# W_G's weight sums moved to the middle block's W_O, a fifth buffer for high halves, another order of k, and a product ahead of the last heads' attention

## The chip, the cores and the metric

The kernel runs on one core of a Trainium2 chip. The metric is the device time of one launch in microseconds, as the median of several runs. The engines are named PE (matrix products), DVE (vector), ACT (scalar), POOL (GpSimd) and SP (which here only issues transfers). Each engine works through its own instructions in program order; it waits on semaphores that the others, and the transfers, raise.

## The reference

One layer over 2112 tokens (2048 of a prompt and 64 of a sample, which start from states of their own), model width 1024, all in float32:

```
h = rms_norm(x, g_pre);  proj = h @ w_in            # ten column groups of 1024: vA bA cA zA q f iv zB gA gB
yA = (silu(zA) * bA * causal_conv3(cA * vA)) @ w_a_out                    # path a
S, o = hgrn2_scan(S0, silu(q) * scale, 1 - fg, iv, log(fg))               # path b: 8 heads, chunks of 64
yB = (norm(o) * g_onorm * silu(zB)) @ w_b_out
out = (sigmoid(gA) * yA + sigmoid(gB) * yB) @ w_o                         # W_O
x = x + rms_norm(out, g_post)
gate = sigmoid(rms_norm(x, g_ple) @ w_ple_gate)                           # W_G
x = x + (p @ w_ple_proj) * gate
```

Outputs are the new x of both sequences, the last two rows of the convolution's input and the last states of the scan.

## The kernel before

**Products.** A float32 product is made of three float32r products: every operand is split into a high half (an ACT cast) and a low half (a DVE subtraction, line 207), and PE adds high by high, high by low and low by high (lines 382 to 384 in sgroup, 549 to 551 in mm3). Most weight matrices are multiplied by a scheme of Strassen's kind: sgroup takes two column blocks of weights and needs seven products instead of eight, for which both sides need sums, four for the activations (T1 to T4, from operands) and four for the weights (S1 to S4, from prepare_sums). The rest (W_O in the first two blocks, a few heads) goes through mm3 directly.

**Blocks.** The tokens are cut into three blocks of 768, 704 and 640 columns, named first, middle and last here. Each block runs path_b (eight heads: head_prep makes the head's projections, head_attn its attention in steps), path_a (eight groups), merge (W_A, W_B and the gates), W_O (final_out), and final_norm. Between blocks the next one's operands are made: `operands` has four steps, i = 0 to 3, and each loads two tiles of x (x_fm, line 665, on POOL's queue), scales them (line 715), makes the sums (697 to 700) and splits them (207). `gates` yields the next block's first groups, sgroups that fill PE while final_norm's chain of small steps runs. In the last block W_O runs group by group inside the merge, and the gate product W_G of the middle and of the last block, which uses the sums of W_G, comes at the end.

**Weight sums.** prepare_sums(firsts, ahead) works group by group, four groups for each matrix. A group loads four weight tiles of 128 x 512 (line 339), makes S1, S3, S2 and S4 on DVE (lines 356, 358, 360, 362), stores each (345), splits it (ACT cast and DVE subtraction at 207) and stores its low half (348). All its transfers, 12 of 256 KB in each group, go through POOL's queue; without `ahead` the next group's loads come behind the former group's stores:

```
            if not ahead and n + 1 < len(groups):
                nxt = load(*groups[n + 1])
            yield
```

The generator is advanced by hooks. Before, path_a of the last block advances the one for W_G (`side`, from its group j = 3 on), as path_a of the middle block does for W_O.

**W_O of the middle block.** final_out calls gemms, which makes the outputs j = 0 and 1 together (gemm_late), 2 to 5 one by one, and 6 and 7 by k. Each output has two halves of 352 columns, and each takes eight k of three matmuls, 384 matmuls in all. The operand of k is the merged row block k; k = 3 and its neighbours are ready last, since the merge makes rows g and g + 4 together. `late` (3 here, 7 in the first block) tells gemm_late which k to leave to the end; that part is issued with the priority of a later place. The copies at line 1185 take the finished PSUM banks to xo[j], ACT squares them (660) and DVE adds the squares (661). At j = 1, 3, 5 and 7 one step of the next block's operands is issued.

**Order and buffers.** The program is written with generators and a list of hooks (`hooks`, `spread_out`): each product of a group calls one hook, which advances whatever stands first in the list; a None in it is a product with nothing attached. The framework then assigns buffers and orders each engine's instructions by priority. Weights come on SP's queue (line 217 the raw ones, 238 the stored low halves) into `raw` (5 buffers), are cast to `hi` on ACT (line 237; 4 buffers by the pool's default) and have their low half in `lo` (4) or `s` (3). `ring` holds 47 activation tiles ("r" in the profile) of 772 columns. PSUM has five banks for products (`pg`) and three for attention (`pa`). In head_attn the lines 951 and 953 are transposes on PE, which read what DVE made at 429.

Of the kernel before, what the change touches and what calls it, by code (L numbers as in the profile page):

```python
# [11 lines left out]
F32R = mybir.dt.float32r  # L12
# [6 lines left out]
P = 128  # L19
D = 1024  # L20
KB = D // P
# [11 lines left out]
W_A, W_B, W_O, W_G = 80, 88, 96, 104  # L33
# [3 lines left out]
CUT = SIZES[0] + SIZES[1] - DEC  # L37
BMAX = max(SIZES)
HMAX = BMAX // 2
RING = 47  # L40
HALVES = 9

LEAD = 7
# [40 lines left out]
def hybrid_step(  # L84
# [22 lines left out]
    wp = ctx.enter_context(tc.tile_pool(name="wp", bufs=4))  # L107
    ring = ctx.enter_context(tc.tile_pool(name="ring", bufs=RING))
# [7 lines left out]
    def nm(s):  # L116
        uid[0] += 1
        return f"{s}_{uid[0]}"
# [20 lines left out]
            yield  # L139

    def rt(n=None, dt=F32):
        return ring.tile([P, BMAX + 4], dt, tag="r", name=nm("r"))[:, : n or wide[0]]

    def hf(n=None):
        return ring.tile([P, HMAX], F32, tag="hf", name=nm("hf"), bufs=HALVES)[:, : n or wide[0] // 2]
# [85 lines left out]

    def split_w(raw, key=None, queue=SP):

        hi = wp.tile([P, 4, P], F32R, tag="hi", name=nm("hi"))
        if key in lows:
            lo = low_tile()
            A.copy(hi, raw)  # L237
            SP.dma_start(lo.bitcast(F32), lows[key])
            return hi, lo
        lo = wp.tile([P, 4, P], F32R, tag="lo", name=nm("lo"))  # L240
        split(raw, hi, lo)
        if key is not None:
            lows[key] = dram.tile([P, 4, P], F32, tag=f"lo{key}", name=nm("low"), bufs=1)
            queue.dma_start(lows[key], lo.bitcast(F32))
        return hi, lo
# [321 lines left out]
    def gemm_late(idxs, act, segs, late):  # L567

        ws = [load_w(i) for i in idxs]
        pss = [[ps_gemm() for _ in segs] for _ in idxs]  # L570
        ks = [k for k in range(KB) if k != late] + [late]
        for part in (ks[:-1], ks[-1:]):
            with placed() if len(part) == 1 else nullcontext():
                for row, w in zip(pss, ws):
                    for ps, s in zip(row, segs):
                        for k in part:
                            mm3(ps, w, act, k, cols_of(s), ks)
        return pss
# [460 lines left out]
    def path_b(bl, hc, first, kept, fills, hs):  # L1039


        def keep_z(hd, z):
            kept["o", hd] = spill("o", hd)
            G.dma_start(kept["o", hd], z)

        for hd in range(NH):
            d = head_prep(bl, hc, hd, first, hs)
            if not (first and hd == 0):
                next(fills, None)
            assert not hooks  # L1050
            attn = [head_attn(i, gs, d, hd) for i, gs in enumerate(bl["parts"])]
            hooks.extend([None] * 3 if first and hd == 0 else [])
            for step in range(4):
                hooks.extend(partial(next, g) for g in attn)
                if step == 2:
                    hooks.extend([None] * (2 if first and hd == 0 else 1))
            hooks.append(partial(keep_z, hd, d["z"]))
# [8 lines left out]
    def ple(bl, ph, kept, held=None, shared=False):  # L1066


        for j in range(KB):
            if held is not None:  # L1070
                hi, lo = held[j]
            else:
                raw = wp.tile([P, 4, P], F32, tag="raw", name=nm("raw"), bufs=5)[:, :2, :]
                SP.dma_start(raw, w_ple[j])
                with tc.high_priority():
                    hi = wp.tile([P, 4, P], F32R, tag="hi", name=nm("hi"))[:, :2, :]
                    lo = low_tile()[:, :2, :]
                    A.copy(hi, raw)
                    SP.dma_start(lo.bitcast(F32), lows["p", j])
            t = rt()  # L1080
            for s in bl["segs"]:
                pp, c = ps_attn()[:, : s["n"]], cols_of(s)
                for k, (xhi, xlo) in enumerate(ph):
                    T.matmul(pp, hi[:, k, :], xhi[:, c], start=k == 0, stop=False)
                    T.matmul(pp, hi[:, k, :], xlo[:, c], start=False, stop=False)
                    last[0] = T.matmul(pp, lo[:, k, :], xhi[:, c], start=False, stop=k == 1).ins
                with tc.high_priority():
                    if shared and j < 4 and s is bl["segs"][1]:
                        V.tensor_copy(t[:, c], pp)
                    else:  # L1090
                        copied = copies[0] = A.copy(t[:, c], pp).ins
            if bl["last"]:
                kept["p", j] = t
            else:
                kept["p", j] = spill("p", j)
                G.dma_start(kept["p", j], t)
                if not shared:
                    lows["p", j] = dram.tile([P, 2, P], F32, tag=f"lop{j}", name=nm("low"), bufs=1)
                    SP.dma_start(lows["p", j], lo.bitcast(F32))
            with behind_all((copied,) if hooks else ()):  # L1100
                hook()
            yield
# [298 lines left out]
    for bi, bl in enumerate(blocks):  # L1401
# [6 lines left out]
        nxt = None if bl["last"] else blocks[bi + 1]  # L1408
        cols, a_first = [], []
        rows = of_block(nxt, row_rstd(nxt, cols)) if nxt else iter(())  # L1410
        sums_ahead = prepare_sums((W_A, W_B), True) if first else prepare_sums((W_O,) if nxt else (W_G,), False)

        def side(rows, sums_):
            for j in range(KB):
# [42 lines left out]
        if nxt:  # L1457
            hc = new_operands()
            with width_of(nxt):
                ops = of_block(nxt, operands(hc, spread_all(cols), partial(load_x, nxt)))  # L1460
            for j, _ in enumerate(final_out(segs, mg, xo, acc, KB - 1 if first else KH - 1)):
                if j in (1, 3, 5, 7):
                    run(ops, 1)
            fills = of_block(nxt, gates(nxt, hc, kepts[bi + 1], False))
            norm = of_block(bl, final_norm(bl, segs, xo, acc, h2, kept, not first))
            spread_out((norm, (0, 1, 0, 1) + (0, 1, 0) * KB + (0, 1, 0, 1) + (0, 1) * KB))
            run(fills, LEAD)
            assert not hooks
            if first:
                run(final_gate(bl, segs, h2, kept))  # L1470
        else:
            spread_out((norms[0], (3, 0, 0, 1, 1, 2, 2, 2, 2)), (norms[1], (0, 1, 1, 0, 1, 1, 2, 2, 2, 1, 1, 2, 2, 2, 2)))
            raws = load_p(bl, G)
            gate = final_gate(blocks[bi - 1], blocks[bi - 1]["segs"], rows2, kepts[bi - 1], SP)
            for j, _ in enumerate(of_block(blocks[bi - 1], gate)):
                if j == 3:
                    ph = [split_rt(raw) for raw in raws]
            run(ple(bl, ph, kept))
            assert not hooks
            first_rows = [narrow(half(t, 0)) for t in h2[:KH]]  # L1480
            run(in_turn([gate_in_turn(bl, h2, xo, kept)], first_rows))
# [49 lines left out]
```

## Time and profile before

| | us |
|---|---|
| median of 3 runs (2616.6 to 2618.29) | 2617.77 |
| the profiled execution | 2618.3 |
| its span, first to last instruction | 2616.6 |
| PE busy (99% of the span) | 2584.3 |
| DVE busy (63%) | 1648.8 |
| ACT busy (58%) | 1525.9 |
| POOL busy (14%) | 376.6 |

The granted clock of PE is 0.998 over the span, and the DMA engines moved 747 MB at 285 GB/s. The chain that ended last is PE for 82%, DMA for 5%, ACT for 4% and DVE for 3%. W_O of the middle block starts at 1694.6 us and the first gates of the last block follow it at about 1761; the last block's heads lie between 1882 and 2130, its path_a between 2130 and some 2330. A row of the timeline gives the start, the duration, the engine, the line of the program, the operation with its output and input tiles, and in brackets how long the engine had stood idle and what released it. Matmuls are pipelined: a row's duration is longer than the distance to the next start.

### The profile page before, as it was taken

Reading aid. Unit: us, or ns where it says so; the run is one execution under the profiler, and the core shown is the slowest. Engines: PE = TensorE matmul, PEld = TensorE weight load, DVE = VectorE, ACT = ScalarE, POOL = GpSimd, SP = SyncE. Lnnn points to the kernel's source line nnn. Section 1 sums busy time; section 2 is a strip of 40 time slices with the busy share of each in tenths; the row PEclk is TensorE's granted clock in tenths of the full one; section 3 lists DMA queues with packets and bytes.
Section 4 is the critical chain, followed back from the end, with each engine's and each line's share of the span. In section 5 each row is a group of like instructions: output and inputs, shape, how many; then the busy total and the mean of one; then the engine's idle time right before and its main releaser. Section 6 shows DMA issues by size and latency. Waiting matters only on the chain.

```text
span 2616.6 us, 47076 instructions
## 1 busy us (share of the span) xinstructions
PE 2584.3 (99%) x16432; PEld 2564.4 (98%) x16432; DVE 1648.8 (63%) x3165; ACT 1525.9 (58%) x2908; POOL 376.6 (14%) x698
## 2 busy tenths in 40 slices
PE   8999999999999999999999999999999999999999
PEld 8999999999999999999999999999999999999999
DVE  8687788788757655445554557845344444568776
ACT  6666576554433564567775546546677755556746
POOL 1000000110144021210011221002100000211110
PEclk9999999999999999999999999999999999999999
DMA  7677677788788698876768998859977779999977
GB/s 274 220 262 265 232 247 263 274 302 268 267 330 286 233 379 284 279 242 223 229 224 296 364 381 304 305 167 377 366 252 244 245 254 332 381 335 359 344 264 264
DMA packets 362095, 747.01 MB, mean 285 GB/s; under 512 B 44513, under 2 KB 49153, under 8 KB 361857
## 3 DMA queue, kind: packets, MB, share of 16 engines
q1 hardware_dynamic: 319680, 579.81, 64.2%
q0 software_dynamic: 41888, 164.15, 17.2%
q8 instruction: 129, 2.11, 0.3%
q14 instruction: 110, 0.89, 0.1%
q10 hardware_dynamic: 288, 0.05, 0.0%
HBM read 532.26 MB, written 211.57 MB: 284 GB/s over the span
## 4 chain that ended last, share of the span: by engine, by line
PE 82%; DMA 5%; ACT 4%; DVE 3%; issue 2%; POOL 1%; ACTq 0%; POOLq 0%; SPq 0%; DVEq 0%
PE pg L382 16%; PE pg L383 16%; PE pg L384 16%; PE pg L551 5%; PE pg L550 5%; PE pg L549 5%; PE pg L516 4%; PE pg L517 4%; PE pg L518 3%; DMA raw<-S 2%; DMA r<-w_blk 1%; PE pa L984 1%; PE pa L1020 1%; PE pa L970 1%; ACT hi L237 1%
## 5 line engine op out<-in xcount | busy, mean ns | idle before, releaser
L382 PE MATMUL pg<-r,hi 128*128 128x320 f32 (+2 forms) x3304 | 1087.5, 329 | 5.5 <-DVE r L429 3.8
L383 PE MATMUL pg<-r,hi 128*128 128x320 f32 (+2 forms) x3304 | 1069.3, 324 | 0.0
L384 PE MATMUL pg<-r,lo 128*128 128x384 f32 (+2 forms) x2356 | 766.9, 326 | 4.1 <-DMA lo<-low 4.1
L237 ACT CAST hi<-raw 128x512 fp32r<-128x512 f32 x720 | 442.9, 619 | 465.5 <-PE pg L383 137.2
L382 PEld LDWEIGHTS pg<-r,hi 128*128 128x128 f32 x3304 | 622.6, 188 | 7.9 <-issue 4.7
L383 PEld LDWEIGHTS pg<-r,hi 128*128 128x128 f32 x3304 | 622.7, 188 | 0.2 <-DVE r L207 0.2
L384 PEld LDWEIGHTS pg<-r,lo 128*128 128x128 f32 x2356 | 443.2, 188 | 5.1 <-DMA lo<-low 5.1
L384 PE MATMUL pg<-r,s 128*128 128x352 f32 (+1 forms) x948 | 299.3, 316 | 1.0 <-DMA s<-low 1.0
L549 PE MATMUL pg<-r,hi 128*128 128x384 f32 (+1 forms) x768 | 256.1, 334 | 1.6 <-ACT r L207 1.6
L550 PE MATMUL pg<-r,hi 128*128 128x384 f32 (+1 forms) x768 | 256.1, 334 | 0.1
L207 ACT CAST hi<-raw 128x512 fp32r<-128x512 f32 x218 | 134.7, 620 | 178.2 <-PE pg L550 57.9
L207 DVE TENSOR_TENSOR r<-r,r 128x320 fp32r<-128x320 f32 (+7 forms) x298 | 182.0, 633 | 64.9 <-ACT r L207 63.9
L551 PE MATMUL pg<-r,lo 128*128 128x384 f32 (+1 forms) x656 | 219.9, 335 | 0.0
L517 PE MATMUL pg<-r,hi 128*128 128x320 f32 (+1 forms) x672 | 211.1, 316 | 0.2 <-DVE r L207 0.2
L516 PE MATMUL pg<-r,hi 128*128 128x320 f32 (+1 forms) x672 | 206.0, 316 | 0.9 <-ACT r L207 0.8
L207 DVE TENSOR_TENSOR lo<-raw,hi 128x512 fp32r<-128x512 f32 x218 | 149.3, 686 | 63.1 <-ACT hi L207 60.4
L207 ACT CAST r<-r 128x320 fp32r<-128x320 f32 (+7 forms) x298 | 161.0, 576 | 46.0 <-DVE r L715 12.7
L207 ACT CAST hi<-s 128x512 fp32r<-128x512 f32 x160 | 98.0, 618 | 145.7 <-PE pg L383 130.8
L384 PEld LDWEIGHTS pg<-r,s 128*128 128x128 f32 x948 | 178.5, 188 | 1.8 <-DMA s<-low 1.8
L396 ACT COPY hf<-pg 128x352 f32<-128x352 f32 (+2 forms) x354 | 156.7, 444 | 3.8 <-PE pg L384 3.6
L207 DVE TENSOR_TENSOR lo<-s,hi 128x512 fp32r<-128x512 f32 x160 | 110.1, 689 | 68.9 <-ACT hi L207 67.3
L549 PEld LDWEIGHTS pg<-r,hi 128*128 128x128 f32 x768 | 144.8, 189 | 2.2 <-ACT r L207 2.2
(365 smaller groups left out, 4097.7 us busy)
## 6 DMA issues: line engine op xcount, KB each, us to landing
raw<-w_blk SPq DMA_DIRECT2D x570, 256.0 KB, 4.2
lo<-low SPq DMA_DIRECT2D x411, 256.0 KB, 4.6
raw<-S SPq DMA_DIRECT2D x408, 256.0 KB, 4.4
low<-lo SPq DMA_DIRECT2D x314, 256.0 KB, 3.5
s<-low SPq DMA_DIRECT2D x309, 256.0 KB, 4.5
S<-s SPq DMA_DIRECT2D x152, 256.0 KB, 3.2
r<-w_blk POOLq DMA_DIRECT2D x64, 256.0 KB, 6.8
S<-r POOLq DMA_DIRECT2D x64, 256.0 KB, 5.8
```

The lines of the kernel that those rows point to most:

```text
L207: return A.copy(hi, src).ins, V.tensor_tensor(lo, src, hi.bitcast(F32), ALU.subtract).ins
L237: A.copy(hi, raw)
L382: add(hi[:, k, :], xhi, start=start and k == 0, stop=False)
L383: add(hi[:, k, :], xlo, start=False, stop=False)
L384: last[0] = add(lo[:, k, :], xhi, start=False, stop=k == KH - 1).ins
L396: copied = A.copy(got[n], ps[bank])
L516: add(hi[:, k, :], xhi, start=start and k == 0, stop=False)
L517: add(hi[:, k, :], xlo, start=False, stop=False)
L518: last[0] = add(lo[:, k, :], xhi, start=False, stop=k == KH - 1).ins
L549: T.matmul(ps, hi[:, k % 4, :], xhi[:, c], start=k == ks[0], stop=False)
L550: T.matmul(ps, hi[:, k % 4, :], xlo[:, c], start=False, stop=False)
L551: last[0] = T.matmul(ps, lo[:, k % 4, :], xhi[:, c], start=False, stop=k == ks[-1]).ins
```

## The change

It has four parts. The generator for W_G's sums is no longer advanced by the last block's path_a: a new one, gate_sums, is advanced in the middle block's W_O, at j = 0 (the first group's loads) and j = 2 to 5 (a group each). `hi` has a fifth buffer, of 2 KB a partition, and `ring` pays for it with one tile fewer and two columns less in each. gemm_late takes the k in the order from late + 1 on, so 4, 5, 6, 7, 0, 1, 2, 3 in the middle block, where it was 0, 1, 2, 4, 5, 6, 7, 3; in the first block, with late = 7, it stays 0 to 7. In the last block, where a head has two parts, one None goes ahead of the attention's hooks, so that they start a product later. Besides, the plan of hooks for final_norm is shifted in a few places.

```diff
--- before.py
+++ after.py
@@ -37,7 +37,7 @@
 CUT = SIZES[0] + SIZES[1] - DEC
 BMAX = max(SIZES)
 HMAX = BMAX // 2
-RING = 47
+RING = 46
 HALVES = 9
 
 LEAD = 7
@@ -139,7 +139,7 @@
             yield
 
     def rt(n=None, dt=F32):
-        return ring.tile([P, BMAX + 4], dt, tag="r", name=nm("r"))[:, : n or wide[0]]
+        return ring.tile([P, BMAX + 2], dt, tag="r", name=nm("r"))[:, : n or wide[0]]
 
     def hf(n=None):
         return ring.tile([P, HMAX], F32, tag="hf", name=nm("hf"), bufs=HALVES)[:, : n or wide[0] // 2]
@@ -231,7 +231,7 @@
 
     def split_w(raw, key=None, queue=SP):
 
-        hi = wp.tile([P, 4, P], F32R, tag="hi", name=nm("hi"))
+        hi = wp.tile([P, 4, P], F32R, tag="hi", name=nm("hi"), bufs=5)
         if key in lows:
             lo = low_tile()
             A.copy(hi, raw)
@@ -568,7 +568,7 @@
 
         ws = [load_w(i) for i in idxs]
         pss = [[ps_gemm() for _ in segs] for _ in idxs]
-        ks = [k for k in range(KB) if k != late] + [late]
+        ks = [(late + 1 + k) % KB for k in range(KB)]
         for part in (ks[:-1], ks[-1:]):
             with placed() if len(part) == 1 else nullcontext():
                 for row, w in zip(pss, ws):
@@ -1049,7 +1049,7 @@
                 next(fills, None)
             assert not hooks
             attn = [head_attn(i, gs, d, hd) for i, gs in enumerate(bl["parts"])]
-            hooks.extend([None] * 3 if first and hd == 0 else [])
+            hooks.extend([None] * (3 if first and hd == 0 else int(bl["last"] and len(attn) == 2)))
             for step in range(4):
                 hooks.extend(partial(next, g) for g in attn)
                 if step == 2:
@@ -1073,7 +1073,7 @@
                 raw = wp.tile([P, 4, P], F32, tag="raw", name=nm("raw"), bufs=5)[:, :2, :]
                 SP.dma_start(raw, w_ple[j])
                 with tc.high_priority():
-                    hi = wp.tile([P, 4, P], F32R, tag="hi", name=nm("hi"))[:, :2, :]
+                    hi = wp.tile([P, 4, P], F32R, tag="hi", name=nm("hi"), bufs=5)[:, :2, :]
                     lo = low_tile()[:, :2, :]
                     A.copy(hi, raw)
                     SP.dma_start(lo.bitcast(F32), lows["p", j])
@@ -1408,7 +1408,8 @@
         nxt = None if bl["last"] else blocks[bi + 1]
         cols, a_first = [], []
         rows = of_block(nxt, row_rstd(nxt, cols)) if nxt else iter(())
-        sums_ahead = prepare_sums((W_A, W_B), True) if first else prepare_sums((W_O,) if nxt else (W_G,), False)
+        sums_ahead = prepare_sums((W_A, W_B), True) if first else prepare_sums((W_O,), False) if nxt else iter(())
+        gate_sums = prepare_sums((W_G,), False) if nxt and not first else iter(())
 
         def side(rows, sums_):
             for j in range(KB):
@@ -1459,11 +1460,13 @@
             with width_of(nxt):
                 ops = of_block(nxt, operands(hc, spread_all(cols), partial(load_x, nxt)))
             for j, _ in enumerate(final_out(segs, mg, xo, acc, KB - 1 if first else KH - 1)):
+                if j in (0, 2, 3, 4, 5):
+                    next(gate_sums, None)
                 if j in (1, 3, 5, 7):
                     run(ops, 1)
             fills = of_block(nxt, gates(nxt, hc, kepts[bi + 1], False))
             norm = of_block(bl, final_norm(bl, segs, xo, acc, h2, kept, not first))
-            spread_out((norm, (0, 1, 0, 1) + (0, 1, 0) * KB + (0, 1, 0, 1) + (0, 1) * KB))
+            spread_out((norm, (0, 1, 0, 0, 1) + (0, 1, 0) * (KB - 1) + (0, 1) + (0, 1, 0, 0, 1) + (0, 1) * KB))
             run(fills, LEAD)
             assert not hooks
             if first:
```

On POOL the 48 transfers of the sums come into the queue between the loads of x. Before, in the middle block's W_O (line 1107 loads earlier gates, 665 the x of the next operands):

```order
L1107 DMA r_4710_19930<-g9__3134_13105 128x704
L665 DMA r_4845_20597<-x_fm 128x640
L665 DMA r_4846_20600<-x_fm 128x640
L665 DMA r_4876_20760<-x_fm 128x640
L665 DMA r_4877_20763<-x_fm 128x640
L665 DMA r_4907_20923<-x_fm 128x640
```

And now, the stretch of that queue around the second operand pair (groups 1 and 2 of the sums):

```order
L348 DMA low_4906_20834<-r_4907_20836 128x512
L339 DMA r_4908_20840<-w_blk 128x512
L339 DMA r_4909_20841<-w_blk 128x512
L339 DMA r_4910_20842<-w_blk 128x512
L339 DMA r_4911_20843<-w_blk 128x512
L665 DMA r_4912_20848<-x_fm 128x640
L665 DMA r_4913_20851<-x_fm 128x640
L345 DMA S1_4933_20944<-r_4910_20842 128x512
L345 DMA S3_4936_20952<-r_4909_20841 128x512
```

The loads of pair i = 1 stood directly behind those of pair 0; now 24 transfers of the sums stand between the two pairs, another 20 ahead of pairs 2 and 3, and group 0's four loads ahead of pair 0.

On ACT, before, around the copies of W_O's output j = 4 (the two rows of line 1185, which free two PSUM banks; the 640-wide casts at 207 belong to pair 1):

```order
L237 CAST hi_4922_20958<-raw_4921_20956 128x512
L207 CAST r_4883_20779<-r_4880_20770 128x640
L207 CAST r_4885_20783<-r_4877_20763 128x640
L1185 COPY r_4895_20849<-pg_4893_20799 128x352
L1185 COPY r_4895_20849<-pg_4894_20824 128x352
```

And now:

```order
L207 CAST r_4904_20828<-r_4882_20732 128x512
L207 CAST r_4907_20836<-r_4885_20735 128x512
L237 CAST hi_4992_21130<-raw_4991_21128 128x512
L237 CAST hi_5016_21277<-raw_5015_21275 128x512
L207 CAST r_4914_20854<-r_4912_20848 128x320
L207 CAST r_4917_20863<-r_4915_20857 128x640
L207 CAST r_4919_20867<-r_4916_20858 128x640
L207 CAST r_4921_20871<-r_4913_20851 128x640
L1185 COPY r_4931_20937<-pg_4929_20887 128x352
L1185 COPY r_4931_20937<-pg_4930_20912 128x352
```

Pair 1's casts stand ahead of the copies in both programs; the casts of the sums' group 1 (the 512-wide rows at 207) now stand ahead of them as well, and the x tiles that the casts read (r_4912 and r_4913) are the loads that moved on POOL.

On PE, before, at the attention of one of the last block's heads (lines 382 to 384 are the group's first product, 951 and 953 the transposes):

```order
L382 MATMUL pg_5638_24064<-r_4938_21086,hi_5618_24024 128x320
L383 MATMUL pg_5638_24064<-r_4938_21086,hi_5618_24024 128x320
L384 MATMUL pg_5638_24064<-r_4938_21086,lo_5619_24025 128x320
L951 MATMUL pa_5640_24079<-ident_75,r_5579_23846 128x128 x4
L953 MATMUL pa_5641_24080<-ident_75,r_5581_23848 128x128 x4
```

And now:

```order
L382 MATMUL pg_5704_24239<-r_5005_21255,hi_5685_24190 128x320
L383 MATMUL pg_5704_24239<-r_5006_21256,hi_5685_24190 128x320
L384 MATMUL pg_5704_24239<-r_5005_21255,s_5686_24191 128x320
L951 MATMUL pa_5706_24254<-ident_75,r_5643_24006 128x128 x4
L953 MATMUL pa_5707_24255<-ident_75,r_5645_24008 128x128 x4
```

The transposes stood behind the first product of the next group and stand behind its second now, twelve matmuls later.

## The prediction

> **What bounds the kernel now.** I read the page's busy lines first, then the waits of PE, then its timeline wherever its pace broke, and last the queues of POOL, ACT and DVE around those places.
>
> ```profile
> PE 2584.3 (99%) x16432; PEld 2564.4 (98%) x16432; DVE 1648.8 (63%) x3165; ACT 1525.9 (58%) x2908; POOL 376.6 (14%) x698
> ```
>
> PE sets the end: work on another engine costs nothing until PE stands still. The profiled execution took 2618.3 us, 0.5 above the median of the three shown (2617.77); the sum is made against 2618.3, and 0.5 comes off at its end. A bubble on PE costs more than its idle time, as the start of the middle block's W_O shows (start, duration, engine, line, tiles, idle before):
>
> ```profile
> 1697.74 0.32 PE L550 MATMUL pg<-r,hi 128*128 128x352 f32 x1
> 1697.90 0.32 PE L551 MATMUL pg<-r,lo 128*128 128x352 f32 x1
> 1698.59 0.43 PE L549 MATMUL pg<-r,hi 128*128 128x352 f32 x1 [0.36 <-ACT r L207]
> ...
> 1700.97 0.58 PE L549 MATMUL pg<-r,hi 128*128 128x352 f32 x2 [1.23 <-ACT r L207]
> ...
> 1703.09 0.50 PE L550 MATMUL pg<-r,hi 128*128 128x352 f32 x1
> 1703.38 0.50 PE L551 MATMUL pg<-r,lo 128*128 128x352 f32 x1
> ...
> 1704.85 0.35 PE L549 MATMUL pg<-r,hi 128*128 128x352 f32 x1
> ```
>
> Ahead of this the matmuls start 0.16 apart; after the 1.23 us wait they start 0.29 apart until 1704.85. Idle and slow stretch together lose 4.2 us: (1704.85 − 1697.90) less 17 matmuls at 0.161. So a wait of over a microsecond carries about 1.7 us of slow matmuls behind it.
>
> **What the change takes away.** (a) *W_O's first wait.* With the late half last of all, k runs 4, 5, 6, 7, 0, 1, 2, 3 where it ran 0, 1, 2, 4 to 7, 3: the halves that ACT casts last are needed about 12 matmuls later. 12 × 0.161 = 1.9 us against 0.36 + 1.23 of idle: the whole 4.2 goes.
>
> (b) *W_G's sums in the last block's path_a.* Stretches of 50 us, PE alone (length, busy and matmuls, granted clock, DMA share, GB/s), then what the engines waited for from 2235 to 2305 (us, times, longest):
>
> ```profile
> 2200.00:2250.00 50.00, 49.30 (x337) 1.00 0.99 365
> 2250.00:2300.00 50.00, 46.25 (x301) 0.97 1.04 393
> 2300.00:2350.00 50.00, 50.00 (x342) 1.00 0.91 320
> ```
>
> ```profile
> DVE r L356 <- DMA r<-w_blk: 17.8, 3, 6.4
> PE pg L382 <- DVE r L429: 3.2, 3, 1.8
> ```
>
> ```profile
> 2237.27 0.69 DVE L356 TENSOR_TENSOR r<-r,r 128x512 f32<-128x512 f32 x1 [5.01 <-DMA r<-w_blk]
> ```
>
> DVE stands at L356 for the sums' loads, PE waits for the L429 queued behind it, and DMA is full. Against the third stretch the first two lack 5 + 41 matmuls, at 50 / 342 = 0.146 us each: 6.7 goes (6 to 7.2).
>
> (c) *The last heads' transposes.*
>
> ```profile
> 1959.10 0.60 PE L951 MATMUL pa<-ident,r 128*128 128x128 f32 x4
> 1959.90 0.84 PE L953 MATMUL pa<-ident,r 128*128 128x128 f32 x4 [0.20 <-DVE r L429]
> 1960.57 0.39 PE L969 MATMUL pa<-r,hf 128*128 128x128 f32 x2
> ```
>
> ```profile
> L953 PE MATMUL pa<-ident,r 128*128 128x128 f32 x40 | 8.6, 292 | 2.0 <-DVE r L429 2.0
> ```
>
> From L951 to L969 it is 1.47 us, where eight transposes 0.11 apart (four end after 0.60, the last 0.27 long) would take 0.9: 0.6 a head, up to 0.7 with the slower start behind it, in seven of the last block's eight heads; the group row has their idle time, 2.0 in all from 1882 to 2130. Twelve matmuls of 0.146, 1.75 us, now stand ahead of these transposes, more than DVE's L429 is late: 4.2 to 5.2 goes, I take 4.7.
>
> (d) *The fifth buffer.* One plain case stands in the trace:
>
> ```profile
> 910.83 0.43 PE L382 MATMUL pg<-r,hi 128*128 128x352 f32 x1 [0.74 <-ACT hi L237]
> ```
>
> 1.0 goes. At 1766 PE lost 1.3 behind a cast of the same kind:
>
> ```profile
> 1767.61 0.42 PE L382 MATMUL pg<-r,hi 128*128 128x320 f32 x1 [0.93 <-ACT hf L396]
> ```
>
> but there the copy L396 stays queued behind that cast in the new order, so I take nothing. One ring slot fewer (46) pays for the buffer; I count it in the waits below. At 1800 a late low half costs PE 2.17 of idle:
>
> ```profile
> 1802.56 0.41 PE L384 MATMUL pg<-r,lo 128*128 128x320 f32 x1 [2.17 <-DMA lo<-low]
> ```
>
> DMA is full there with or without the sums (1761:1851 below); a later PE may find it loaded: 0 to 4.8, I take 1. Together (a) to (d): 4.2 + 6.7 + 4.7 + 1.0 + 1.0 = 17.6 (14 to 22).
>
> **What it adds: 48 transfers, 32 DVE and 16 ACT instructions inside W_O.** Nothing new in kind, so the question is who queues behind them. Length, PE, PEld, DVE, ACT and POOL busy, clock, DMA share, GB/s:
>
> ```profile
> 1694.00:1761.00 67.00, 65.28 (x394) 64.11 (x392) 32.20 (x54) 30.15 (x57) 3.75 (x7) 0.97 0.52 175
> 1761.00:1851.00 90.00, 85.92 (x574) 84.40 (x573) 46.51 (x77) 55.44 (x106) 21.24 (x37) 0.98 1.00 376
> ```
>
> By busy time there is room: 32 × 0.7 (L356 above) = 22 us of DVE, 10 of ACT and 12.6 MB beside the 11.7 (24.3 MB in 67 us is 363 GB/s). But the four groups are a chain: a group's loads stand in POOL's queue behind the former group's stores, and those behind its DVE sums. And x_fm's operand pair i=1, whose loads POOL had issued by 1698.68, now stands behind the loads of group 2, pairs 2 and 3 behind all 48.
>
> ```profile
> 1698.68 0.54 POOL L665 DMA_DIRECT2D r<-x_fm  x1 [2.62 <-DVE r L207]
> 1791.04 0.54 POOL L665 DMA_DIRECT2D r<-x_fm  x1 [3.95 <-DMA g__4994_21301<-r]
> ```
>
> The last row also shows a POOL transfer held until an earlier one has landed. What hurts: on ACT, pair 1's four casts stand ahead of L1185, the copy of output j=4 that frees two PSUM banks, and matmul 312 of W_O's 384 waits for that copy; this was so before too, but the pair had been loaded long since.
>
> ```profile
> 1717.28 0.89 DVE L661 TENSOR_TENSOR r<-r,r 128x704 f32<-128x704 f32 x1 [13.07 <-ACT r L660]
> 1718.09 1.67 DVE L715 SCALAR_TENSOR_TENSOR r<-r,vec,r 128x640 f32<-128x640 f32 x2
> ...
> 1723.43 2.30 DVE L207 TENSOR_TENSOR r<-r,r 128x640 fp32r<-128x640 f32 x3 [0.38 <-ACT r L207]
> ...
> 1732.53 0.88 DVE L715 SCALAR_TENSOR_TENSOR r<-r,vec,r 128x640 f32<-128x640 f32 x1
> ...
> 1735.96 0.49 DVE L700 TENSOR_TENSOR r<-r,r 128x320 f32<-128x320 f32 x1
> ```
>
> The chain, from t = 0 at W_O's first matmul (1694.6), PE free at 0.161 per matmul. DVE's L661 of j=1 comes at 1717.28, less the 4.2 of (a): t = 18.5; group 0's L356 follows at 19.3. Its four sums, pair 0's operands (1718.1 to 1725.7 in the trace, 7.6 us) and four lows, whose ACT casts stand behind weight casts paced by PE, end at 34; POOL issues group 1's loads by 36. What they take to land lies between these rows (KB, median us):
>
> ```profile
> r<-x_fm POOLq DMA_DIRECT2D x6, 320.0 KB, 4.2
> raw<-S SPq DMA_DIRECT2D x4, 256.0 KB, 3.0
> S<-r POOLq DMA_DIRECT2D x64, 256.0 KB, 5.8
> ```
>
> ```profile
> DMA to landing us min/median/max: 2.9/6.8/9.6
> ```
>
> The first two are W_O's own at a DMA share of 0.52; the third is the sums' stores and the last their 64 loads (line 339), over the whole run. With the sums in it W_O lies between; I take 5, from 2.9 to 6.8. Landed at 40.5, sums and lows 5.6 (eight × 0.7): 46; group 2's loads to 48; pair 1 issued at 49, held by stores on their way. Group 2's three first sums stand ahead on DVE, from 53 to 55.2; then L715 to L700 of pair 1 (3.9 us in the trace) and L362, 0.7; ACT's last cast and L1185 about 1.5 later: 61. PE is there at 312 × 0.161 = 50.2. **First wait 10.5**; two landings in a row count, so 2 × 2.1 less at 2.9 and 2 × 1.8 more at 6.8: 6.3 to 14.1.
>
> From its end, R, the rest repeats: group 2's lows and stores and group 3's loads are issued by R + 6.5 and landed at R + 11.5, its sums and lows take 5.6, and pair 2 is issued at R + 17; landed 4.2 later, it is through L715 (0.9) and reaches its first cast at R + 22.3. PE comes to the first gate that reads it 78 matmuls on, 12.6, with the slow start at R + 14. **Second wait 8.3** (4.9 to 12), and 3.3 more where the next product waits for the L1185 behind pair 2's other three casts and the DVE sums that feed them. Two slow starts at 1.7 are 3.4. W_O's bill: 10.5 + 8.3 + 3.3 + 3.4 = 25.5 (18 to 33).
>
> The page "DMA: Bandwidth & Descriptors" of the Trainium skill (section "Anatomy of one DMA — SWDGE (gpsimd) path") fits a GpSimd-issued DMA as 2.0 us plus bytes over 436e3, which is an estimate of 2.6 us for these 256 KB. The rows above, 5.8 and 6.8 in the median, disagree; by its figure the sum would be that of the rival "quick landing".
>
> **The sum.** 25.5 − 17.6 = +7.9: 2626.2 for an execution like the profiled one, 2625.7 as a median. Ends: 18 − 22 = −4, 33 − 14 = +19: 2614 to 2637.
>
> **Rivals.** *Quick landing*: every transfer takes 2.9, since W_O's queues are half idle. Then 6.3 + 4.9 + 3.3 + 3.4 = 17.9, and 17.9 − 17.6 = +0.3: 2618.6, no change. For it: share 0.52, 3.0 for raw<-S. Against: 5.8 and 6.8 for these very transfers. *W_O hides the sums* (the other side): DVE is idle for 13.07 us ahead of 1717.28, ACT for 37 of W_O's 67; if group 0's chain runs that early and pair 1 is issued by t = 38, no PSUM bank is late and 17.6 is gained whole: 2600.2; it decides as soon as the W_O bill falls below 12.4. Against: L356 stands behind L661, which stood at 1717.28 for ACT. *Crowding*: the pairs and stores that leave W_O late run into 1761:1851 at a share of 1.00, where low halves already come late (2.17 above); two more such waits with their slow starts, 2 × (2.2 + 1.7), make it +15.7: 2633.5. *The change does not do what it says*: the fifth buffer and the free product leave their waits where they are: 5.7 more than forecast, 2631.4.
>
> **Chances.** Forecast 0.50, crowding 0.14, buffer or product without effect 0.07, quick landing 0.13, hidden 0.16. A measurement of this kernel tells 0.2%, 5.2 us, from no change. Of the forecast's 0.50, whose own range is 2614 to 2637, 0.40 lies above +5.2, 0.09 within and 0.01 below −5.2; of quick landing's 0.13, 0.10 within and 0.03 below. So slower 0.40 + 0.14 + 0.07 = 0.61, within 0.2% 0.19, faster 0.16 + 0.03 + 0.01 = 0.20. The range, 2606 to 2638, holds all but the far part of the hidden case and the worst of crowding.
>
> **What would show it.** In the changed kernel's trace: L549 in W_O waiting about 10 us for ACT L1185 (PE's waits between 40 and 60 us after W_O's start) and L382 waiting for ACT's L207 right behind W_O; POOL's x_fm rows in the middle of L345 and L348 rows; no wait at W_O's first matmuls; L953 without DVE L429; 342 matmuls rather than 301 in each 50 us of the last path_a. It is wrong if W_O takes 67 us or less, or if the waits that (a) to (d) remove are still there.

## The result, and the profile after

| | before | after |
|---|---|---|
| median, us | 2618.03 (4 runs, 2616.6 to 2618.31) | 2661.92 (4 runs, 2661.47 to 2663.19) |
| the profiled execution | 2618.3 | 2663.2 |
| its span | 2616.6 | 2661.5 |
| PE busy | 2584.3 | 2590.7 |

The ratio is 1.017 (95% interval 1.0152 to 1.0187): 44 us slower. The forecast was slower too, but 2625.7, and 2661.92 lies far outside its range of 2606 to 2638.

What PE waited for over the whole run, in us, times, and the longest, the largest five that the kernel before did not have:

```profile
PE pg L549 <- ACT r L1185: 14.2, 1, 14.2
PE pg L382 <- ACT r L207: 11.0, 1, 11.0
PE pg L551 <- DVE lo L207: 8.2, 4, 3.1
...
PE pg L384 <- DVE lo L207: 5.3, 1, 5.3
...
PE pg L382 <- ACT r L1185: 2.2, 1, 2.2
```

The first two and the last stand where they were expected, in the middle block's W_O (first matmul at 1720.49) and right behind it. On the timeline:

```profile
1785.47 0.66 PE L549 MATMUL pg<-r,hi 128*128 128x352 f32 x1 [14.16 <-ACT r L1185]
...
1811.02 0.64 PE L382 MATMUL pg<-r,hi 128*128 128x320 f32 x1 [10.96 <-ACT r L207]
1812.39 0.63 PE L383 MATMUL pg<-r,hi 128*128 128x320 f32 x1 [0.73 <-DVE r L207]
1815.45 0.63 PE L382 MATMUL pg<-r,hi 128*128 128x320 f32 x1 [2.17 <-ACT r L1185]
```

The other two, low halves of weights that DVE makes, belong to a place that the prediction does not name: the gate product W_G at the end of the first block (line 551) and the product right behind it (line 384). Both programs issue the same products there; the stretches of the changed kernel (length, PE, PEld, DVE, ACT and POOL busy, clock, DMA share, GB/s):

```profile
1000.00:1050.00 50.00, 48.61 (x279) 47.97 (x277) 17.25 (x27) 15.46 (x28) 6.45 (x12) 1.00 0.61 200
1050.00:1110.00 60.00, 45.54 (x221) 43.63 (x222) 20.38 (x33) 11.90 (x24) 11.81 (x22) 0.86 0.67 212
```

and of the kernel before:

```profile
1000.00:1050.00 50.00, 50.00 (x288) 50.00 (x287) 23.88 (x37) 15.38 (x28) 9.14 (x17) 1.00 0.81 263
1050.00:1085.00 35.00, 35.00 (x208) 35.00 (x207) 14.46 (x23) 11.51 (x22) 9.17 (x17) 1.00 0.84 299
```

500 matmuls take 110 us where 496 took 85, so some 25 us are lost here. The shares of DMA, DVE and ACT over the whole stretch are lower than before: something has become serial. POOL's queue shows it, in the changed kernel:

```profile
1019.26 0.54 POOL L1107 DMA_DIRECT2D r<-p  x1 [5.83 <-DVE r L1259]
1019.78 0.55 POOL L1260 DMA_DIRECT2D y_fm<-r  x1
1024.36 0.54 POOL L1107 DMA_DIRECT2D r<-x  x1 [4.03 <-DMA y_fm<-r]
1032.02 0.54 POOL L1107 DMA_DIRECT2D r<-p  x1 [7.12 <-DVE r L1259]
```

and before:

```profile
1024.88 0.54 POOL L1260 DMA_DIRECT2D y_fm<-r  x1 [1.85 <-DVE r L1259]
1025.41 0.54 POOL L1107 DMA_DIRECT2D r<-x  x1
1032.42 0.54 POOL L1107 DMA_DIRECT2D r<-p  x1 [6.47 <-issue]
```

For each output final_gate reloads a tile of p and one of x, multiplies p by the gate (1258), adds x (1259) and stores (1260). Before, three tiles go round: the next x is loaded right behind the store, into the tile that 1259 has just read, and only the p after that waits for the store to land. With one ring tile fewer the x waits until that store has landed, p's next load waits until 1259 has read x, and an output takes 12.8 us (1019.26 to 1032.02) where it took 8.4 (48 matmuls at 50 / 288 = 0.174). DVE stands at 1259 for x, and the weights' low halves, which PE needs, stand behind it on DVE:

```profile
1018.00 0.96 DVE L1259 TENSOR_TENSOR r<-r,r 128x768 f32<-128x768 f32 x1 [1.99 <-DMA r<-x]
1019.49 0.69 DVE L207 TENSOR_TENSOR lo<-raw,hi 128x512 fp32r<-128x512 f32 x1 [0.53 <-PE pg L551]
...
1030.77 0.96 DVE L1259 TENSOR_TENSOR r<-r,r 128x768 f32<-128x768 f32 x1 [5.86 <-DMA r<-x]
1031.64 0.68 DVE L207 TENSOR_TENSOR lo<-raw,hi 128x512 fp32r<-128x512 f32 x1
```

What was to be removed is removed. The last path_a, 44 us later than before (length, PE busy, clock, DMA share, GB/s), and the last heads' transposes:

```profile
2244.00:2294.00 50.00, 50.00 (x343) 1.00 0.91 300
2294.00:2344.00 50.00, 50.00 (x343) 1.00 0.92 300
```

```profile
L953 PE MATMUL pa<-ident,r 128*128 128x128 f32 x40 | 7.0, 272 | 0.0
```

### The profile page after: what moved, and what is told of

Read it like the earlier page. It is cut to its first block, busy times and chain, and to the rows that moved or that the text cites. A ratio compares the mean times of both kernels' runs of the same rounds, so it can differ in the third digit from the quotient of the medians.

```text
span 2661.5 us, 47044 instructions
## 1 busy us (share of the span) xinstructions
PE 2590.7 (97%) x16432; PEld 2570.9 (97%) x16432; DVE 1649.8 (62%) x3165; ACT 1525.8 (57%) x2908; POOL 378.8 (14%) x698
## 4 chain that ended last, share of the span: by engine, by line
PE 46%; DMA 5%; issue 4%; DVE 2%; POOL 1%; ACT 1%; SPq 0%; POOLq 0%; ACTq 0%; DVEq 0%
PE pg L382 10%; PE pg L383 10%; PE pg L384 10%; PE pg L517 3%; PE pg L516 3%; PE pg L518 3%; DMA r<-w_blk 1%; DMA raw<-S 1%; DMA lo<-low 1%; PE pa L1022 1%; PE pa L984 1%; PE pa L1020 1%; PE pa L970 1%; DMA raw<-w_blk 1%; PE pg L551 1%
## 5 line engine op out<-in xcount | busy, mean ns | idle before, releaser
L237 ACT CAST hi<-raw 128x512 fp32r<-128x512 f32 x720 | 442.5, 619 | 451.2 <-PE pg L383 178.6
L382 PEld LDWEIGHTS pg<-r,hi 128*128 128x128 f32 x3304 | 624.0, 189 | 22.1 <-ACT r L207 11.4
L383 PEld LDWEIGHTS pg<-r,hi 128*128 128x128 f32 x3304 | 624.3, 189 | 1.2 <-DVE r L207 1.2
L549 PE MATMUL pg<-r,hi 128*128 128x384 f32 (+1 forms) x768 | 257.8, 336 | 14.7 <-ACT r L1185 14.2
L207 ACT CAST hi<-raw 128x512 fp32r<-128x512 f32 x218 | 134.8, 620 | 170.2 <-PE pg L383 67.8
L207 DVE TENSOR_TENSOR r<-r,r 128x320 fp32r<-128x320 f32 (+7 forms) x298 | 182.0, 632 | 55.7 <-ACT r L207 53.3
L207 ACT CAST r<-r 128x320 fp32r<-128x320 f32 (+7 forms) x298 | 161.7, 576 | 84.9 <-DVE r L715 30.0
L207 DVE TENSOR_TENSOR lo<-raw,hi 128x512 fp32r<-128x512 f32 x218 | 149.5, 687 | 59.7 <-PE pg L551 26.8
L207 ACT CAST hi<-s 128x512 fp32r<-128x512 f32 x160 | 98.2, 618 | 121.9 <-PE pg L383 84.5
L549 PEld LDWEIGHTS pg<-r,hi 128*128 128x128 f32 x768 | 145.8, 190 | 15.3 <-ACT r L1185 14.5
L550 PEld LDWEIGHTS pg<-r,hi 128*128 128x128 f32 x768 | 146.0, 190 | 0.4 <-DVE r L207 0.4
```

Source lines behind the costliest of these rows:

```text
L207: return A.copy(hi, src).ins, V.tensor_tensor(lo, src, hi.bitcast(F32), ALU.subtract).ins
L382: add(hi[:, k, :], xhi, start=start and k == 0, stop=False)
L383: add(hi[:, k, :], xlo, start=False, stop=False)
L549: T.matmul(ps, hi[:, k % 4, :], xhi[:, c], start=k == ks[0], stop=False)
L550: T.matmul(ps, hi[:, k % 4, :], xlo[:, c], start=False, stop=False)
```

## The experiments

The times of the kernel before on the chips of these runs lay between 2612.6 and 2621.1, their median between 2615.6 and 2616.9; ratios are to runs of it on the same chips.

**46 tiles alone.**

```diff
-RING = 47
+RING = 46
...
-        return ring.tile([P, BMAX + 4], dt, tag="r", name=nm("r"))[:, : n or wide[0]]
+        return ring.tile([P, BMAX + 2], dt, tag="r", name=nm("r"))[:, : n or wide[0]]
```

> The kernel before with one change alone: the ring has 46 tiles of 770 columns instead of 47 of 772 (the high halves keep four buffers). Theory 'ring': the gate product at the end of the first block needs three free tiles (x, p, and the next p) and gets two, so x and p are loaded one after the other; PE loses about 26 us between 1010 and 1135, DVE waits at L1259 for r<-x, and the time is 2640 to 2648. Rival 'casts': the loss comes from the other order that the fifth buffer gives to the casts on ACT and DVE; then this kernel takes 2616 to 2621.

Measured 2638.51, ratio 1.0086 (1.0066 to 1.0106): 22 us for one tile, a little under the range. The view of line 1259 has the wait (us, times) in this kernel; the kernel before has none there:

```profile
  DMA r<-x: 23.0, 7
```

"Casts" falls. The loss in the first block is larger than 22: W_O of the middle block starts at 1719.29 us, 24.7 later than before (1694.58). Some 4 us come back at W_O's first matmuls, where this kernel loses 0.2 us and the kernel before 4.2, although its order of k is the old one; what sets that is taken up under (a) below.

**46 tiles at their old width, and the fifth buffer.**

```diff
-RING = 47
+RING = 46
...
-        hi = wp.tile([P, 4, P], F32R, tag="hi", name=nm("hi"))
+        hi = wp.tile([P, 4, P], F32R, tag="hi", name=nm("hi"), bufs=5)
...
```

> The kernel before with the fifth buffer for high halves and 46 tiles in the ring, at their old width of 772 columns; nothing else changed. Theory 'ring': the number of tiles is what costs, not their width, and the fifth buffer gives back at most 2 us (the wait of 0.74 for a cast at 910): 2635 to 2641, with DVE waiting at L1259 for r<-x in the first block's gate product, as in the run with 46 tiles alone (2638.5). Rival 'width': the narrower tiles or their addresses were the cost: 2614 to 2620. Rival 'buffer pays': the fifth buffer gives back 5 us or more elsewhere: 2633 or less.

Measured 2639.19, ratio 1.0087 (1.0067 to 1.0107), within the noise of the run before: the old width and the fifth buffer together change nothing that can be told from the times (each by itself was not measured), and "width" and "buffer pays" fall. The wait of 0.74 for a cast at 910 is gone here and in the changed kernel; PE waits 0.21 for a copy instead:

```profile
910.27 0.43 PE L382 MATMUL pg<-r,hi 128*128 128x352 f32 x1 [0.21 <-ACT hf L396]
```

**The change without its fifth buffer.** The changed kernel with `RING = 47`, tiles of 772 columns and four buffers.

> The changed kernel without the fifth buffer: 47 tiles of 772 columns and four buffers for high halves, all else as changed. Theory 'ring': the 26 us of the first block are gone, W_O's waits for L1185 (14.2) and for ACT's L207 (11.0) stay: 2633 to 2639. Rival 'one tile in W_O': W_O's waits, too, come from the tile that is missing; then they shrink to a few us and the time is below 2620.

Measured 2642.63, ratio 1.0102 (1.0081 to 1.0122), 4 us above the range. The first block's loss is gone, and W_O's waits are nearly what they were:

```profile
PE pg L549 <- ACT r L1185: 13.4, 1, 13.4
PE pg L382 <- ACT r L207: 11.7, 1, 11.7
```

19 us came back rather than 26, in good part because the loss at W_O's first matmuls, 0.4 us in the changed kernel, is 3.4 again here, with the same order of k. So it hangs on more than that order.

**W_G's sums in W_O alone.** The kernel before, with these lines:

```diff
-        sums_ahead = prepare_sums((W_A, W_B), True) if first else prepare_sums((W_O,) if nxt else (W_G,), False)
+        sums_ahead = prepare_sums((W_A, W_B), True) if first else prepare_sums((W_O,), False) if nxt else iter(())
+        gate_sums = prepare_sums((W_G,), False) if nxt and not first else iter(())
...
+                if j in (0, 2, 3, 4, 5):
+                    next(gate_sums, None)
```

> The kernel before with W_G's sums in the middle block's W_O and nothing else changed. Theory 'chain': the sums alone make W_O's two waits, 14 and 11 us with what follows them, some 30 to 34 us in all, and the last path_a gains 6.7 to 7.2: 2640 to 2646, or a little less where the wait at W_O's first matmuls is absorbed. Rival 'mixture': the sums alone cost little (under 10 us) and only the new order of k makes their casts late: 2612 to 2622.

Measured 2647.75, ratio 1.0121 (1.0101 to 1.0141), 2 us above the range. PE waits 14.8 for L1185 and 11.6 for ACT's L207. The chain needs no help from the rest of the change.

**The order of k and the free product alone.**

```diff
-        ks = [k for k in range(KB) if k != late] + [late]
+        ks = [(late + 1 + k) % KB for k in range(KB)]
...
-            hooks.extend([None] * 3 if first and hd == 0 else [])
+            hooks.extend([None] * (3 if first and hd == 0 else int(bl["last"] and len(attn) == 2)))
```

> The kernel before with the new order of k and the free product ahead of the last heads' attention, and nothing else: 47 tiles, four buffers, W_G's sums in the last path_a. By the prediction's terms (a) and (c) 4.2 and 4.7 go: 2607 to 2611. Rival: the waits only move to the next product, and under 3 us go: 2615 to 2618.

Measured 2609.37 (10 runs), ratio 0.9975 (0.9965 to 0.9985), and once more, beside the last runs told below:

> The kernel before with the new order of k and the free product once more (2609.4 before), beside the three others on the same chip: 2606 to 2612.

2610.49 (10 runs), ratio 0.998 (0.9971 to 0.9989). L953 no longer waits in either, and the last heads are some 4.8 us shorter in both. What PE loses at W_O's start is 0.4 us in the first profiled execution and 3.0 in the second, so the free product's gain is the sure one; what the order of k gives by itself was not measured.

**The norm's plan of hooks** with these two (the diff's last pair of lines).

> The kernel before with the new order of k, the free product and the changed plan of hooks for the norms; 47 tiles, four buffers, W_G's sums in the last path_a. The norm's own waits (L624 and L640) are 0.3 to 0.7 us each, so the plan should change under 2 us against the 2609.4 without it: 2607 to 2611. Rival: the plan takes the late low halves behind W_O along (5.7 us in the run without it): 2604 to 2606.

Measured 2610.78 (10 runs), ratio 0.998 (0.9971 to 0.999): no effect that can be told.

**Two groups in W_O, two in path_a**, with k and the free product; prepare_sums got bounds for its list of groups.

```diff
-        groups = [(idx + g, idx + KH + g) for idx in firsts for g in range(KH)]
+        groups = [(idx + g, idx + KH + g) for idx in firsts for g in range(KH)][lo:hi]
...
-        sums_ahead = prepare_sums((W_A, W_B), True) if first else prepare_sums((W_O,) if nxt else (W_G,), False)
+        sums_ahead = prepare_sums((W_A, W_B), True) if first else prepare_sums((W_O,) if nxt else (W_G,), False, 2 if not nxt else 0)
+        gate_sums = prepare_sums((W_G,), False, 0, 2) if nxt and not first else iter(())
```

> The kernel before with the new order of k and the free product (2609.4 measured), 47 tiles, and two of W_G's four sum groups in the middle block's W_O (at j = 0, 2 and 3, as changed), the other two in the last path_a. Theory 'chain': the groups run one behind the other, and what is late in W_O is what stands behind the third and the fourth; with two, pair 1 goes right behind group 1's lows, the wait for L1185 falls from 13.4 to 5 to 9 and the second wait (11.7) is gone; path_a keeps half its 6.9: 2612 to 2619. Rival 'share': the loss grows with the transfers and sums in W_O in proportion, half of some 36: 2622 to 2628.

Measured 2624.95 (5 runs, 2618.45 to 2625.28), ratio 1.0024 (1.0009 to 1.0039). The second wait is gone, and path_a with two groups has no wait of PE at all; but the first wait is still there:

```profile
1761.69 0.66 PE L549 MATMUL pg<-r,hi 128*128 128x352 f32 x1 [11.21 <-ACT r L1185]
```

The time fits "share", the pattern fits "chain" with a first wait set too low. Another 4.4 us are lost at W_O's first matmuls.

**Pairs ahead of sums.** The change with 47 tiles; at each j the operands' step is issued before the sums' step.

```diff
+                if j in (1, 3, 5, 7):
+                    run(ops, 1)
                 if j in (0, 2, 3, 4, 5):
                     next(gate_sums, None)
-                if j in (1, 3, 5, 7):
-                    run(ops, 1)
```

> The changed kernel with 47 tiles and four buffers (2642.6 measured), and one step further: in W_O each operand pair is issued ahead of the sums' group of the same j, so that pair 1's loads stand in front of group 1's sums on POOL instead of behind group 2's loads, and pair 2 in front of group 3's sums instead of behind all 48. Theory 'chain': the first wait (13.4 us for L1185) ends or falls under 4, since pair 1 is issued about 10 us earlier; the second (11.7 for ACT's L207) falls to 3 to 8, since pair 3 is now the late one: 2620 to 2630. Rival 'crowding': the waits come from DMA and DVE being shared, wherever the pairs stand; both stay above 10 us and the time above 2636.

Measured 2640.77, ratio 1.0093 (1.007 to 1.0115). The longest wait for L1185 in W_O fell from 13.4 to 3.6, as "chain" had it, but the time did not: 2.4, 3.6, 7.1 and 5.1 us of waits stand where there were 13.4 and 11.7, and W_O's first matmuls lose 6.4 rather than 3.4. With four groups the chain is longer than W_O (in the changed kernel the last group's last low half is issued 83 us after W_O's first matmul, and W_O took 66 before), so the pairs' order seems only to say where PE pays.

**Both together**: two groups, and pair 1 ahead of group 1's sums, which come at j = 4 rather than 3.

```diff
                 if j in (1, 3, 5, 7):
                     run(ops, 1)
+                if j in (0, 2, 4):
+                    next(gate_sums, None)
```

> As the run with two sum groups in W_O and two in path_a (2624.9, one wait of 11.2 us for L1185), but pair 1's loads stand ahead of group 1's sums on POOL, its operands ahead of them on DVE and ACT, and the sums are advanced at j = 0, 2 and 4. Theory 'pair 1': what holds L1185, and so the PSUM bank, is pair 1's casts waiting for loads behind a sums group; the wait falls under 3 us, path_a loses under 2: 2602 to 2612, and below the kernel before. Rival 'casts': the ACT casts of the sums themselves hold L1185; the wait stays above 7 us and the time above 2617.

Measured 2614.37 (10 runs), ratio 0.9997 (0.9987 to 1.0006): above the range, and no faster than the kernel before. What PE waits for at L1185 is 1.1 us in W_O, as the theory had it, and 3.2 behind it, which it had not:

```profile
PE pg L382 <- ACT r L1185: 3.2, 1, 3.2
...
PE pg L549 <- ACT r L1185: 1.1, 1, 1.1
```

This run alone does not tell pair 1 from the sums' casts, since these stand behind the copies of output j = 4 here and stood ahead of them in the run with two groups. That run's trace tells: ACT was done with group 1's casts at 1746.7, and then stood 9.1 us for pair 1's L715 on DVE, which needs the loads, before it could cast pair 1 and come to the copies:

```profile
1756.88 0.46 ACT L207 CAST r<-r 128x320 fp32r<-128x320 f32 x1 [9.10 <-DVE r L715]
```

So it was pair 1. POOL issued its loads in the run with both at

```profile
1736.38 0.54 POOL L665 DMA_DIRECT2D r<-x_fm  x1
1737.34 0.54 POOL L665 DMA_DIRECT2D r<-x_fm  x1 [0.42 <-ACT hi L237]
```

and in the run with two groups and the sums first twelve us later:

```profile
1748.58 1.08 POOL L665 DMA_DIRECT2D r<-x_fm  x2
```

**Group 1's sums later still**, at j = 5 in place of 4.

> As the run before last (two groups in W_O, pair 1 ahead of group 1), with group 1's sums at j = 5, behind pair 2 rather than ahead of it. Theory 'pair 1': pair 2 then isn't late either and the rest of the waits in W_O goes: 0 to 4 us below that run. Rival: group 1's lows now reach into the first gates' stretch, where DMA is full, and cost 3 us or more there.

Measured 2618.33 (10 runs), ratio 1.0013 (1.0004 to 1.0022): 4 us above the run before, as the rival had it. Pair 2 is in time now, but pair 3's loads stand behind group 1's lows on POOL, and PE waits 3.0 for its cast; L1185 still costs 2.0. The late low halves behind W_O, which the rival had in mind, cost no more than in the run before (2.7 us against 1.4 and 1.9).

**One group in W_O** (loads at j = 0, sums at j = 3), three in path_a.

> The new order of k and the free product, 47 tiles, one of W_G's sum groups in W_O (loads at j = 0, sums at j = 3 behind pair 1) and three in the last path_a. Theory 'pair 1': pair 1 stands behind nothing but group 0's four loads and stores, so no wait for L1185; three groups in path_a lose 0 to 5 (four lost 6.9, two 0.3): 2603 to 2611. Rival 'casts': a wait of 4 us or more in W_O even so: above 2613.

Measured 2611.64 (10 runs), ratio 0.9987 (0.9978 to 0.9997). PE has no wait for L1185, path_a lost 1.8 us. Without any group in W_O it is 2610.49 on the same chip: moving one group costs about as much as it brings.

**Loads issued ahead in W_O** (`prepare_sums((W_G,), True)`, 47 tiles).

> The changed kernel with 47 tiles and four buffers (2642.6 measured), where a group's loads in W_O are issued ahead of the former group's sums' end and its lows go through the three small weight buffers instead of ring tiles. Theory 'chain': each group's period (22, 15 and 20 us from first store to first store in the changed kernel) loses the 5 to 8 us of landing, the waits for L1185 and ACT's L207 together fall from 25 to 10 to 18: 2627 to 2637. Rival 'buffers': the ring and the small buffers that the weights need too hold the loads back, and the time stays above 2639.

Measured 2644.37, ratio 1.0107 (1.0087 to 1.0128). The rival is right. The longest wait is now for an earlier output's L1185, and the lows take the small buffers that weights need:

```profile
PE pg L549 <- ACT r L1185: 20.4, 1, 20.4
PE pg L551 <- DMA s<-low: 10.2, 4, 7.7
```

ACT stands for such a buffer itself, with the copies queued behind:

```profile
1752.08 1.24 ACT L207 CAST s<-r 128x512 fp32r<-128x512 f32 x2 [10.33 <-DMA low<-s]
```

**The sums in the last heads** (a step at each of heads 3 to 7).

> The kernel before with the new order of k and the free product (2609.4 measured), and W_G's sums made in the last block's heads 3 to 7, one group a head of 32 us, instead of its path_a. In the heads DMA is busy for 0.76 and DVE for half the time, no x_fm pair stands behind the sums, and a group's chain of some 25 us fits into a head. Theory: the path_a loss of 6.9 us ends and the heads lose under 2: 2602 to 2605. Rival: the sums' eight tiles or DVE's waits for their loads stop the heads as they stopped path_a, some 7 us or more: 2609 to 2618.

Measured 2622.46 (9 runs), ratio 1.0025 (1.0015 to 1.0036). It is the rival, and more than it had: DVE stands at L356 (25.1 us in three waits), and the attention behind it on DVE keeps PE waiting:

```profile
PE pa L1020 <- DVE att L975: 10.5, 3, 4.8
```

**The sums in path_a on POOL** (lines 356 to 362 as G.tensor_tensor for W_G).

> The kernel before with the new order of k and the free product (2609.4 measured), and W_G's sums in the last path_a as before, but with the four additions and subtractions of a group on POOL instead of DVE (lines 356 to 362), so that POOL, not DVE, stands waiting for the loads. Theory: PE's waits for L429 in path_a (3.2 us idle in the kernel before, 6.9 lost in all) came from DVE standing at L356; they end, and what is left is a late low half of 1.3: 2602 to 2606. Rival: the sums on POOL are so slow, or DMA at a share of 1.0 so full, that the lows and the weights come late all the same: 2608 to 2615.

Measured 2611.45 (10 runs), ratio 0.9975 (0.9966 to 0.9985), no better than without. DVE no longer stands at L356 and PE no longer waits for L429, but low halves come late, and some 4 us are lost at the start of the merge where there was nothing. Why that moved there was not pursued.

## Why the prediction was right and wrong

**The side and the mechanism in W_O were right.** PE waits for L1185 and then for pair 2's casts, 28 us of idle in all (14.16 + 10.96 + 0.73 + 2.17), and the runs with one group, with two, and with the pair moved ahead show that a pair of x_fm behind a sums group is the cause of the first wait. "W_O hides the sums" fell, and so did "quick landing".

**The step that failed is (d).** "One ring slot fewer (46) pays for the buffer; I count it in the waits below": nothing was counted there. The tile by itself costs 24.7 us in the first block, 22 in the whole time, half of all that the change lost, in a place where PE had lost nothing. The trace of before showed the edge. Its waits from 1005 to 1085, where PE has none (us, times, longest):

```profile
DVE r L1258 <- DMA r<-p: 24.4, 6, 6.4
...
POOL r L1107 <- DMA y_fm<-r: 19.9, 5, 6.2
```

POOL's load of p stood waiting for a store to land, so no ring tile was to spare there, and DVE was already waiting for that load. These rows, over a stretch in which PE is busy throughout, are what a missing tile should have been priced from.

**W_O's bill was sized too low.** From W_O's first matmul to the 423rd after it PE took 102.7 us (1720.49 to 1823.21) against 73.0 before: 29.7 more, where 25.5 − 4.2 = 21.3 was forecast. Since 3.8 of (a) went at its start, the sums cost 33.5 there, not 25.5. The issue of pair 1 fell at t = 50 (49 forecast), but the landing took 8.2 and 6.9 us and group 2's loads up to 7.9, where 5 was taken: 14.2 of wait, not 10.5 (the prediction's own 61 − 50.2 is 10.8). The rows 5.8 and 6.8 were the better guide than W_O's own 3.0 and 4.2. By the fit in the Trainium skill's "DMA: Bandwidth & Descriptors" (section "Anatomy of one DMA — SWDGE (gpsimd) path") a load of 256 KB takes 2.6 us, an estimate. This trace disagrees: group 2's loads, of that size, took 6.9 to 7.9 us, in a stretch with a DMA share of 0.78:

```profile
1718.00:1811.00 93.00, 67.75 (x409) 66.88 (x408) 47.23 (x81) 37.23 (x69) 27.38 (x51) 0.89 0.78 272
```

The second wait was 11.0 with 0.7 behind it (8.3 forecast), the third 2.2 (3.3), and the slow stretches behind them some 5.5 (3.4).

The price of a slow start, 1.7 us, was read from one place and is about right, but "a wait of over a microsecond" is not what brings it. In the trace of before PE is granted half its clock for 3.4 us behind the waits of 1.23 us at 1700.97 and 2.17 at 1802.56, which is the 1.7 us, but a wait of 1.30 at 2263.61 is followed by full speed (length, PE busy, granted clock, DMA share, GB/s):

```profile
1701.50:1704.90 3.40, 3.40 (x13) 0.50 0.11 42
1803.90:1807.30 3.40, 3.40 (x15) 0.50 1.04 414
2263.60:2267.00 3.40, 3.39 (x22) 1.00 1.05 393
```

In the run with two groups and pair 1 ahead even the wait of 3.24 has none behind it (clock 1.00 from 1768 to 1772). Which waits bring it stays open.

**(b) and (c)** came as forecast: 343 matmuls in each 50 us of path_a, and L953 without a wait.

**(a)** is gone in the changed kernel (0.4 us left of 4.2), but, as far as the traces tell, by luck and not for the reason given. With 47 tiles and the new order of k 0.4 to 6.4 us are lost at W_O's start in the profiled executions; with 46 tiles and the old order 0.2. The traces show what it goes with. ACT's casts of W_O's weights (L237) stand ahead of its casts of the merged halves (L207), and before, ACT stood there for weights that had not landed:

```profile
1695.47 0.62 ACT L237 CAST hi<-raw 128x512 fp32r<-128x512 f32 x1 [3.19 <-DMA raw<-w_blk]
1696.82 0.62 ACT L237 CAST hi<-raw 128x512 fp32r<-128x512 f32 x1 [0.74 <-DMA raw<-w_blk]
1697.35 0.48 ACT L207 CAST r<-r 128x352 fp32r<-128x352 f32 x1
```

In the run with 46 tiles alone it did not:

```profile
1718.81 0.62 ACT L237 CAST hi<-raw 128x512 fp32r<-128x512 f32 x1 [0.88 <-PE pg L517]
```

In 12 of the 17 traces ACT stands for such a load after W_O's first matmul (the longest such wait is 0.7 to 3.2 us), and PE loses 1.6 to 6.4 us; in the other five it does not, and PE loses 0.2 to 0.5. Both orders of k are in both sets. Why the loads land late in some executions was not followed, and no run changed them.

**(d)**'s other two: the wait at 910 fell from 0.74 to 0.21, so 0.5 us went there, not 1.0; and around 1850 PE still waits 1.05 and 1.76, and nothing of the 1.0 forecast there went.

The bill: +25 in the first block and +30 in W_O, −7 in path_a, −5 at the transposes; the rest, some +1, is in waits of a microsecond or less. The runs with one part alone agree: 46 tiles +22, the sums in W_O +31, the order of k and the free product −7, together +46. They are not quite independent, as W_O's start shows.

## What to carry to other kernels

Before a buffer is bought with a slot of a shared ring, find the stretches where some engine already waits for the ring's stores to land; PE being busy there says nothing about how near the edge is. Here one slot of 47 cost 22 us, where the buffer it paid for returned half a microsecond in the trace and nothing measurable in the time. Work put into a stretch with idle engines costs by what queues behind it in program order, not by busy time: ask which loads now stand behind which stores, and move those first. Of a change in four parts, the two that issue no transfers and take no memory were the ones that paid together, 2609.4 and 2610.5 against 2616.5 and 2616.2 (ratio 0.9975 and 0.998), and of these the free product surely; no other kernel here is clearly faster. A gain that is seen in one profiled execution is not yet the change's: look whether the same wait comes and goes in runs that leave that part alone.

## What the runs showed that was not expected

A wait of 14.16 us on PE was followed by matmuls 0.29 us apart, as after the 1.23 us wait before, and lost about the same 1.7 us by it. The same kernel's executions can differ in one place: the loss at W_O's start was 0.4 us in one profiled execution of the kernel with k and the free product and 3.0 in another, and its ten times spread from 2606.9 to 2615.1, against 2661.5 to 2663.2 for the changed kernel's four.
